# Six groups of seven products in the second layer's FFN, with their weight sums made in HBM by accumulating transfers

## The chip, the core and the metric

The kernel runs on one core of one Trainium2 chip. Its engines are TensorE (PE, and PEld for its weight loads), VectorE (DVE), ScalarE (ACT), GpSimd (POOL) and SyncE (SP), which here only issues transfers; 16 DMA engines carry the transfers of all queues. The metric is the time of one execution on the device in microseconds (us).

## The reference

A decoder of two layers on 256 tokens of width 2048, all in float32. Layer 0 mixes tokens by latent attention of 16 heads, layer 1 by dilated window attention in three groups. Each mixer is followed by an FFN with a convolution over three tokens; the hidden width is 5632, so its first matrix has 2 x 5632 columns, gate and value.

```python
def conv_ffn(h, w_up, conv_w, conv_b, w_down):
    u = h @ w_up
    up = jnp.pad(u, ((0, 0), (CONV_WIDTH - 1, 0), (0, 0)))
    c = conv_b + up[:, 0:S] * conv_w[0]
    for j in range(1, CONV_WIDTH):
        c = c + up[:, j:j + S] * conv_w[j]
    gate, val = c[..., :FFN_HIDDEN], c[..., FFN_HIDDEN:]
    return (jax.nn.silu(gate) * val) @ w_down

for i in range(2):
    x = x + mixer_i(rms_norm(x, attn_norm[i]), ...)
    x = x + conv_ffn(rms_norm(x, ffn_norm[i]), ffn_w_up[i], ffn_conv_w[i], ffn_conv_b[i], ffn_w_down[i])
return rms_norm(x, final_norm)
```

## The kernel before

**Layout.** Features lie on the 128 partitions, tokens along the free axis. The input of a projection is 16 chunks `xs` of 128 features, each a tile of 512 columns: the 256 tokens rounded to the type fp32r (the high part) and beside them what the rounding left (the low part). Weights come from HBM in blocks of 128 output columns: `load` takes a buffer `w` of the pool `wst` (three buffers), issues its transfer on SP's queue, and splits each half of it into `wh` (ScalarE, a copy that rounds) and `wl` (VectorE, the difference), tiles of 128 x 1024 in the pool `wsp` (five buffers). `proj` multiplies a block with 16 chunks: 16 matmuls of 128 x 512 with `wh` and 16 of 128 x 256 with `wl`. That is a *unit*. The helper `unit` issues a projection, then one entry of the list `steps` (small work that is to run in between), then the evacuation of the unit before.

**Norms.** The gain is folded in when `xs` is made; 1/rms is worked out while the first products run. `rstd_x` sums the squares over partitions (TensorE), makes the mean square `ms` (VectorE), and takes its power -0.5 on GpSimd, into `rcol` (L309; `rstd_rank` does so for the ranks of the attention, into `s`, L321). `spread` lays `rcol` out over the partitions by two matmuls into `po` (L296). In the FFN these are the first two entries of `steps`, `col` and `wide`. Apart from the norms GpSimd has a few `memset`s, those of the paddings `upad` of the FFN among them (L802), and at the start some additions.

**The FFN** (`ffn`, run for both layers). The hidden width is 44 blocks `fb`. A plain block takes two units, `up`: gate and value, each a load of 1 MB; the evacuation multiplies with the norm and convolves (`keep`, `conv`). The second matrix is applied in four segments of 10 to 12 blocks (`SEGS`), `down`: 16 units of 640 to 768 KB, each added to the residual. Before each of the last three segments stands a *four* (`SEVEN`, blocks 12, 23 and 34 and the three after each): gate and value of four blocks by seven products instead of eight, in the manner of Strassen and Winograd, over two halves of the tokens, two halves of the input features (each pair of chunks, one even and one odd) and gate against value. Here the tokens are the stationary operand (`xs`, or sums of token and feature halves, `forms`), the weights the moving one, and the results have tokens on the partitions. In each of the 16 steps beside a `down` (`first` and `second`, eight of each), VectorE makes the sums of the weights from one load (`t13`, `t24`; L883 among them) and TensorE runs four or two of the products (L853 to L855, three matmuls for each: high, low, high parts). The product left over (`third`, `s4`) runs in two halves later, and then `turn` transposes the results (16 transposes, L947) and convolves.

**Order.** The program is written in the order above, and Tile's scheduler sets each engine's queue from it by the time at which it takes an instruction to be ready, and by its place in the text. Each queue is run in order.

Of the kernel before, what the change touches and what calls it, by code (L numbers as in the profile page):

```python
# [18 lines left out]
F32 = mybir.dt.float32  # L19
F32R = mybir.dt.float32r  # L20
BF16 = mybir.dt.bfloat16
I32 = mybir.dt.int32
AF = mybir.ActivationFunctionType
# [3 lines left out]
P = 128  # L27
T = 256
# [12 lines left out]
SEGS = ((0, 10), (10, 21), (21, 32), (32, 44))  # L41
HALF = 4 * P
SEVEN = (12, 23, 34)
NEG = -1.0e30


# [6 lines left out]
def trunk_kernel(tc, x_d, pos_d, gain_d, conv_d, const_d, mask_d, wqa_d, wkva_d, wqb_d, wkvb_d, wo_d,  # L53
                 win_d, dwo_d, wup_d, wdn_d, out_d):
    nc = tc.nc
    with ExitStack() as ctx:
# [5 lines left out]
        tab = ctx.enter_context(tc.tile_pool(name="tab", bufs=1))  # L62
        work = ctx.enter_context(tc.tile_pool(name="work", bufs=4))
        small = ctx.enter_context(tc.tile_pool(name="small", bufs=4))
        pp = ctx.enter_context(tc.tile_pool(name="pp", bufs=4, space=PSUM))
        pss = ctx.enter_context(tc.tile_pool(name="pss", bufs=2, space=PSUM))
        pst = ctx.enter_context(tc.tile_pool(name="pst", bufs=1, space=PSUM))
# [3 lines left out]
        def load(src, n, tok=0, cuts=None, after=()):  # L71

            w = wst.tile([P, D], F32, name="w", tag="w")
            cuts = cuts or (0, n)
            for a, b in zip(cuts, cuts[1:]):
                nc.sync.dma_start(w[:, a:b], src[:, a:b])
                if after:
                    after[0]()  # L80
                    after = after[1:]
            parts = []
            for a in range(0, n, WS):
                b = min(n, a + WS)
                wh = wsp.tile([P, WS], F32R, name="wh", tag="wh")
                wl = wsp.tile([P, WS], F32R, name="wl", tag="wl")
                if a < tok:
                    steps = [a] + [c for c in cuts if a < c < b] + [b]
                    for c, e in zip(steps, steps[1:]):
                        h, l = wh[:, c - a:e - a], wl[:, c - a:e - a]  # L90
                        nc.scalar.activation(h, w[:, c:e], AF.Copy)  # L91
                        nc.vector.tensor_sub(l, w[:, c:e], h.bitcast(F32))  # L92
                else:
                    for h, t in enumerate((wh, wl)):
                        src2 = w[:, a + h * WS // 2:a + (h + 1) * WS // 2].rearrange("p (k c) -> p k c", c=T)
                        t4 = t.rearrange("p (k s c) -> p k s c", s=2, c=T)
                        nc.scalar.activation(t4[:, :, 0, :], src2, AF.Copy)
                        nc.vector.tensor_sub(t4[:, :, 1, :], src2, t4[:, :, 0, :].bitcast(F32))
                parts.append((wh, wl))
            return parts  # L100
# [87 lines left out]

        pending = []
        steps = []  # L190

        def nothing():
            pass
# [9 lines left out]
        def unit(project, evacuate):  # L203
            ps = project()
            if steps:
                steps.pop(0)()
            flush()
            pending.append((evacuate, ps))

        def joined(ps):  # L210

            t = work.tile([P, T], F32, name="lo", tag="lo", bufs=2)
            nc.scalar.activation(t, ps[:, T:], AF.Copy)  # L213
            u = work.tile([P, T], F32, name="sum", tag="tmp")
            nc.vector.tensor_add(u, ps[:, :T], t)  # L215
            return u
# [75 lines left out]
        def spread(col, name, pool):  # L292

            ps = pso.tile([P, 512], F32, name="po", tag="po")
            for tt in range(2):
                nc.tensor.matmul(ps[:, ts(tt, P)], col[:, tt:tt + 1].to_broadcast([P, P]), ident,  # L296
                                 start=True, stop=True)
            if pool is None:
                return ps[:, :T]
            t = pool.tile([P, T], F32, name=name, tag=name)  # L300
            nc.vector.tensor_copy(t, ps[:, :T])
            return t

        def rstd_x(paired=False, last=None):
            ps = sumsq("x", paired, last)
            ms = small.tile([P, 2], F32, name="ms", tag="ms")
            nc.vector.tensor_scalar(ms, ps, 1.0 / D, EPS, op0=ALU.mult, op1=ALU.add)
            r = small.tile([P, 2], F32, name="rcol", tag="rcol")
            nc.gpsimd.tensor_tensor(r, ms, negh, op=ALU.pow)  # L309
            return r  # L310
# [38 lines left out]
        def split_to(dst, src):  # L349

            n = src.shape[-1]
            nc.scalar.activation(dst[:, :n], src, AF.Copy)
            nc.vector.tensor_sub(dst[:, n:], src, dst[:, :n].bitcast(F32))

        def split_act(ps):
            o = act.tile([P, 2 * T], F32R, name="a", tag="a")
            split_to(o, ps)
            return o

        def tokens(k, paired=False):  # L360

            return xt[k].rearrange("p (a e) -> p e a" if paired else "p (e a) -> p e a", e=2)
# [428 lines left out]
            out_proj(dwo_d, os, G_FFN + KC, onto=True)  # L791


        def ffn(layer, goff, ready):
            gl = {}
            rb = {}
# [227 lines left out]
            flush()  # L1024


        with tc.tile_pool(name="lat0", bufs=1) as lat, tc.tile_pool(name="att0", bufs=2) as att:
            mla()
        with tc.tile_pool(name="ffn0", bufs=1) as fpool:
# [11 lines left out]
            nc.scalar.activation(xt[c], xt[c], AF.Copy, scale=gains[:, G_FIN + c:G_FIN + c + 1])  # L1041

        with tc.tile_pool(name="ffn1", bufs=1) as fpool:
            ffn(1, G_FFN + KC, final)

        zero = work.tile([P, T], F32, name="zero", tag="lo", bufs=2)
        nc.vector.memset(zero, 0.0)
# [93 lines left out]
```

## Time and profile before

| | |
|---|---|
| device time, median of 3 runs | 2675.28 us (2674.98 to 2675.42) |
| span of the profiled execution | 2673.9 us |
| its own time outside that span | about 1.4 us by the median |
| TensorE busy | 2657.8 us (99%) |
| VectorE busy | 2105.5 us (79%) |
| ScalarE busy | 1639.7 us (61%) |
| GpSimd busy | 24.7 us (1%) |
| transfers of SP's queue | 503.46 MB, 54.9% of the 16 DMA engines' span |

The busy time of an engine is a share of the whole span. The granted clock of TensorE is full in all of the 40 slices. A row of the timeline gives start, duration, engine, line, operation, its output and inputs with shapes and count, and in brackets the engine's idle time before it and what released it. For a stretch of time the busy time of PE, PEld, DVE, ACT and POOL is given in this order, and then the granted clock, the busy share of the DMA engines and the GB/s that they moved.

### The profile page before, as it was taken

Reading aid. Unit: us, or ns where it says so; the run is one execution under the profiler, and the core shown is the slowest. Engines: PE = TensorE matmul, PEld = TensorE weight load, DVE = VectorE, ACT = ScalarE, POOL = GpSimd, SP = SyncE. Lnnn points to the kernel's source line nnn. Section 1 sums busy time; section 2 is a strip of 40 time slices with the busy share of each in tenths; the row PEclk is TensorE's granted clock in tenths of the full one; section 3 lists DMA queues with packets and bytes.
Section 4 is the critical chain, followed back from the end, with each engine's and each line's share of the span. In section 5 each row is a group of like instructions: output and inputs, shape, how many; then the busy total and the mean of one; then the engine's idle time right before and its main releaser. Section 6 shows DMA issues by size and latency. Waiting matters only on the chain.

```text
span 2673.9 us, 40017 instructions
## 1 busy us (share of the span) xinstructions
PE 2657.8 (99%) x15167; PEld 2338.4 (87%) x15167; DVE 2105.5 (79%) x3630; ACT 1639.7 (61%) x2624; POOL 24.7 (1%) x39
## 2 busy tenths in 40 slices
PE   9999999999999999999999999999999999999998
PEld 7998888888888888898888888888888888888887
DVE  7987888898898876676577667667688889889885
ACT  6775666676666764444454444445666667666665
POOL 2000000000000000000000000000000000000000
PEclk9999999999999999999999999999999999999999
DMA  6335555656566565544544544544555575755744
GB/s 246 138 133 203 189 182 193 239 179 224 197 202 227 182 206 198 179 171 170 191 170 164 197 161 174 188 174 160 189 189 175 191 249 171 223 205 189 237 169 147
DMA packets 153553, 506.19 MB, mean 189 GB/s; under 512 B 11024, under 2 KB 86160, under 8 KB 118928
## 3 DMA queue, kind: packets, MB, share of 16 engines
q1 hardware_dynamic: 153072, 503.46, 54.9%
q8 instruction: 119, 1.95, 0.3%
q14 instruction: 74, 0.61, 0.1%
q10 hardware_dynamic: 288, 0.18, 0.0%
HBM read 501.50 MB, written 2.10 MB: 188 GB/s over the span
## 4 chain that ended last, share of the span: by engine, by line
PE 95%; DMA 1%; DVE 1%; issue 0%; ACT 0%; SPq 0%; DVEq 0%; ACTq 0%
PE pp L137 70%; PE pp L165 3%; PE pp L167 3%; PE pp L166 3%; PE ps L855 1%; PE ps L853 1%; PE ps L854 1%; DMA w<-in_wup 1%; PE pp L104 1%; PE pp L106 1%; PE pp L105 1%; PE pp L853 1%; PE pp L854 1%; PE pp L855 1%; PE po L781 1%; PE ps L744 1%
## 5 line engine op out<-in xcount | busy, mean ns | idle before, releaser
L92 DVE TENSOR_TENSOR wl<-w,wh 128x1024 fp32r<-128x1024 f32 (+3 forms) x802 | 881.9, 1110 | 371.0 <-ACT wh L91 228.1
L91 ACT ACTIVATE wh<-w 128x1024 fp32r<-128x1024 f32 (+3 forms) x802 | 770.9, 966 | 370.8 <-PE pp L137 220.7
L137 PE MATMUL pp<-xs,wh 128*128 128x512 f32 x3648 | 855.5, 390 | 0.0
L137 PEld LDWEIGHTS pp<-xs,wh 128*128 128x128 f32 x3648 | 677.1, 188 | 135.8 <-DVE xs L266 0.2
L137 PE MATMUL pp<-xs,wl 128*128 128x256 f32 x3648 | 465.3, 284 | 0.0
L137 PEld LDWEIGHTS pp<-xs,wl 128*128 128x128 f32 x3648 | 455.7, 191 | 9.3
L137 PE MATMUL pp<-a,wh 128*128 128x512 f32 x1920 | 459.7, 390 | 0.0
L137 PEld LDWEIGHTS pp<-a,wh 128*128 128x128 f32 x1920 | 357.7, 188 | 72.6
L137 PEld LDWEIGHTS pp<-a,wl 128*128 128x128 f32 x1920 | 248.1, 191 | 10.2
L137 PE MATMUL pp<-a,wl 128*128 128x256 f32 x1920 | 252.8, 283 | 0.0
L155 DVE TENSOR_TENSOR wl<-w,wh 128x1024 fp32r<-128x1024 f32 x96 | 116.2, 1218 | 62.3 <-ACT wh L154 50.3
L154 ACT ACTIVATE wh<-w 128x1024 fp32r<-128x1024 f32 x96 | 101.6, 1059 | 96.5 <-PE pp L166 50.0
L213 ACT ACTIVATE lo<-pp 128x256 f32<-128x256 f32 x225 | 85.7, 381 | 119.5 <-PE pp L137 119.4
L165 PE MATMUL pp<-wh,xs 128*128 128x512 f32 x384 | 150.0, 391 | 0.0
L167 PE MATMUL pp<-wl,xs 128*128 128x512 f32 x384 | 149.5, 389 | 0.0
L166 PE MATMUL pp<-wh,xs 128*128 128x512 f32 x384 | 149.4, 389 | 0.0
L962 DVE SCALAR_TENSOR_TENSOR cv<-upad,convs,cv 128x256 f32<-128x256 f32 x256 | 121.1, 481 | 18.3 <-ACT cv L958 15.9
L958 ACT ACTIVATE cv<-upad,convs 128x256 f32<-128x256 f32 x128 | 76.4, 598 | 72.7 <-DVE upad L972 71.0
L215 DVE TENSOR_TENSOR sum<-pp,lo 128x256 f32<-128x256 f32 x225 | 94.1, 418 | 0.2
L120 ACT ACTIVATE pp<-x 128x512 f32<-128x512 f32 x144 | 85.1, 591 | 13.6 <-DVE sum L215 6.8
L880 ACT ACTIVATE wh<-w 128x1024 fp32r<-128x1024 f32 x48 | 51.0, 1062 | 60.0 <-PE pp L137 43.0
L167 PEld LDWEIGHTS pp<-wl,xs 128*128 128x128 f32 x384 | 72.1, 188 | 15.0
(299 smaller groups left out, 3154.7 us busy)
## 6 DMA issues: line engine op xcount, KB each, us to landing
w<-in_wup SPq DMA_DIRECT2D x128, 1024.0 KB, 4.8
w<-in_win SPq DMA_DIRECT2D x96, 1024.0 KB, 4.8
w<-in_wup SPq DMA_DIRECT2D x96, 512.0 KB, 5.1
w<-in_win SPq DMA_DIRECT2D x96, 512.0 KB, 4.1
w<-in_wdn SPq DMA_DIRECT2D x64, 704.0 KB, 4.1
w<-in_wdn SPq DMA_DIRECT2D x32, 768.0 KB, 4.2
w<-in_wdn SPq DMA_DIRECT2D x32, 640.0 KB, 5.3
w<-in_wo SPq DMA_DIRECT2D x16, 1024.0 KB, 4.7
```

The costliest lines, as they stand in the source:

```text
L91: nc.scalar.activation(h, w[:, c:e], AF.Copy)
L92: nc.vector.tensor_sub(l, w[:, c:e], h.bitcast(F32))
L120: nc.scalar.activation(dst, chunk.unsqueeze(1).to_broadcast([P, 2, 2, P]), AF.Copy, scale=0.5)
L137: nc.tensor.matmul(ps[:, i * T:], w_k, xs[k][:, :(2 - i) * T], start=(k == 0 and i == own), stop=(k == n - 1), skip_group_check=(i != own))
L154: nc.scalar.activation(wh4, src, AF.Copy)
L155: nc.vector.tensor_sub(wl4, src, wh4.bitcast(F32))
L165: nc.tensor.matmul(ps, xh, wh, start=k == 0, stop=False)
L166: nc.tensor.matmul(ps, xl, wh, start=False, stop=False)
L167: nc.tensor.matmul(ps, xh, wl, start=False, stop=k == KC - 1)
L213: nc.scalar.activation(t, ps[:, T:], AF.Copy)
L215: nc.vector.tensor_add(u, ps[:, :T], t)
L962: nc.vector.scalar_tensor_tensor(o, v, convs[:, cw + j:cw + j + 1], o, op0=ALU.mult, op1=ALU.add)
```

## The change

Layer 0 keeps `ffn`. Layer 1 gets a function of its own, `ffn_ahead`, with twice as many fours.

- **Fours and units.** Six fours, at blocks 12 and 16, 23 and 27, 34 and 38 (`PERIODS`); 12 blocks by units at the start (`FIRST`), and 20 to 22, 31 to 33, 42 and 43 by units between. So 24 units of `up` become three more fours.
- **Halves of a product.** The feature halves are now the lower and the upper eight chunks. Each of the seven products is made on its own, in two halves: `product(i, q)` issues one load of 1 MB (four blocks, 512 columns each, so pieces of 2 KB), four splits, and 12 matmuls of 128 x 512. Its accumulator is one of the two of `ps`. The order is 1, 2, 6, 7, 4, 5, 3, and the results are added into `u` as they come (`use`). `slot` runs what the tables `first`, `downs` and `ups` have for the place after a unit: one half each in the last 12 units of the start, then beside the units of `down`, in the second and third periods 2, 3, 2, 2 halves after the first four.
- **The sums of weights** are read from HBM. For each four, `plan_sums` takes four HBM tiles `t1` to `t4` of 2.1 MB and lists 16 copies of 0.524 MB from `wup` into them and 16 transfers of the same size that add to what is there (`accum_op`): 96 of each in all. `some_ahead`, called at the start of each `load`, hands out one entry at two of five calls after the eighth: a copy on SP's queue, an accumulating transfer, six entries behind its copy, on GpSimd's, in pieces of at most 256 elements.

The diff, cut to what the parts below speak of:

```diff
+FIRST = 12
+PERIODS = ((0, 11, 12, 16, (20, 21, 22)), (11, 22, 23, 27, (31, 32, 33)), (22, 33, 34, 38, (42, 43)))
...
+        hbm = ctx.enter_context(tc.tile_pool(name="hbm", bufs=1, space=bass.MemoryType.DRAM))
...
 def load(src, n, tok=0, cuts=None, after=()):
+            some_ahead()
             w = wst.tile([P, D], F32, name="w", tag="w")
...
+        def plan_sums(layer, fours):
+            copies, adds = [], []
+            for fb0 in fours:
+                t = {i: hbm.tile([4, P, WS], F32, name=f"t{i}_{layer}_{fb0}") for i in (1, 2, 3, 4)}
+                made[layer, fb0] = t
+                last = None
+                for f in range(4):
+                    blk = lambda h, j: wup_d[layer, 2 * (fb0 + f) + h, :, j * WS:(j + 1) * WS]
+                    copies += [(t[i][f], blk(*hj)) for i, hj in ((1, (0, 0)), (3, (1, 1)), (2, (1, 1)), (4, (0, 1)))]
+                    adds += [(t[1][f], blk(1, 0)), (t[3][f], blk(1, 0)), (t[2][f], t[1][f])]
+                    if last:
+                        adds.append(last)
+                    last = (t[4][f], t[2][f])
+                adds.append(last)
+            late = 6
+            for n in range(len(copies) + late):
+                ahead.append((copies[n] if n < len(copies) else None, adds[n - late] if n >= late else None))
+
+        def some_ahead():
+            state["loads"] = state.get("loads", 0) + 1
+            if state["loads"] > 8 and state["loads"] % 5 in (0, 3) and ahead:
+                c, a = ahead.pop(0)
+                if c:
+                    nc.sync.dma_start(*c)
+                if a:
+                    nc.gpsimd.dma_start(*a, accum_op=ALU.add, max_dma_last_dim=WS)
...
+            products = {1: ("a11", (0, 0)), 2: ("a12", (0, 1)), 3: ("s4", (1, 1)), 4: ("a22", 4), 5: ("s1", 1),
+                        6: ("s2", 2), 7: ("s3", 3)}
...
+                def product(i, q):
...
+                    w = wst.tile([P, D], F32, name="w", tag="w")
+                    if isinstance(what, int):
+                        src = t[what][:, :, q * HALF:(q + 1) * HALF]
+                    else:
+                        h, j = what
+                        src = wup_d[layer, 2 * fb0:2 * fb0 + 8].rearrange("(f i) p c -> i f p c", i=2)[h]
+                        src = src[:, :, j * WS + q * HALF:j * WS + (q + 1) * HALF]
+                    nc.sync.dma_start(w.rearrange("p (f c) -> p f c", f=4), src.rearrange("f p c -> p f c"))
...
+                if s == 0:
+                    deal(m, first[12:], [1] * 12)
+                    deal(m, downs[0], (1, 1))
+                else:
+                    put(ups[s - 1], 0, m.pop(0))
+                    put(ups[s - 1], 2, m.pop(0))
+                    deal(m, ups[s - 1][3:], (1, 1, 1))
+                    deal(m, downs[s], (2, 3, 2, 2))
...
+        plan_sums(1, [fb for _, _, one, two, _ in PERIODS for fb in (one, two)])
...
-            ffn(1, G_FFN + KC, final)
+            ffn_ahead(1, G_FFN + KC, final)
```

The queues as they are built. GpSimd's queue before, from the norm of layer 0's input (`rcol_536`) over the two norms of the ranks to that of layer 0's FFN (`rcol_3656`); a name ends in the number of its tile:

```order
L309 TENSOR_TENSOR rcol_536<-ms_534,negh_115 128x2 [waits DVE_49]
L321 TENSOR_TENSOR s2_546<-ms_543,negh_115 128x2 [waits DVE_49]
L321 TENSOR_TENSOR s2_759<-ms_756,negh_115 128x2 [waits DVE_49]
L802 MEMSET upad0_3600 128x2 [waits DMAHW6_49,PE_49,Activation_49]
L802 MEMSET upad1_3602 128x2
L802 MEMSET upad2_3604 128x2
L802 MEMSET upad3_3606 128x2
L309 TENSOR_TENSOR rcol_3656<-ms_3654,negh_115 128x2 [waits DVE_49]
```

The same place in the changed kernel begins so. DMAHW are counters of SP's transfers, DMASW of GpSimd's own:

```order
L344 TENSOR_TENSOR rcol_562<-ms_560,negh_117 128x2 [waits DVE_49]
L225 DMA t1_1_12_119<-in_wup 128x4x256 [waits DMAHW6_49]
L356 TENSOR_TENSOR s2_572<-ms_569,negh_117 128x2 [waits DVE_49]
L225 DMA t3_1_12_121<-in_wup 128x4x256 [waits DMAHW0_49]
L225 DMA t2_1_12_120<-t1_1_12_119 512x256 [waits DMAHW2_49,DMASW0_49]
L225 DMA t1_1_12_119<-in_wup 128x4x256 [waits DMAHW4_49]
L225 DMA t4_1_12_122<-t2_1_12_120 512x256 [waits DMAHW3_49,DMASW2_49]
L356 TENSOR_TENSOR s2_785<-ms_782,negh_117 128x2 [waits DVE_49]
```

and ends so, at the norm of layer 0's FFN, which is now `rcol_3700`:

```order
L225 DMA t2_1_34_136<-t1_1_34_135 512x256 [waits DMAHW0_49,DMASW0_49]
L225 DMA t4_1_34_138<-t2_1_34_136 512x256 [waits DMAHW2_49,DMASW3_49,DMASW2_49]
L225 DMA t1_1_34_135<-in_wup 128x4x256 [waits DMAHW4_49]
L225 DMA t3_1_34_137<-in_wup 128x4x256 [waits DMAHW5_49,DMASW5_49]
L225 DMA t2_1_34_136<-t1_1_34_135 512x256 [waits DMAHW7_49,DMASW4_49]
L225 DMA t4_1_34_138<-t2_1_34_136 512x256 [waits DMAHW1_49,DMASW7_49,DMASW6_49]
L225 DMA t1_1_34_135<-in_wup 128x4x256 [waits DMAHW2_49]
L344 TENSOR_TENSOR rcol_3700<-ms_3698,negh_117 128x2 [waits DVE_49]
```

Between the two pieces stand further transfers of this kind, 73 in all ahead of `rcol_3700` (the memsets of `upad` among them, behind 50); the other 23 follow it.

SP's queue before, from the last heads' weights over the out projection to the first `down` of layer 0; xN stands for N alike in a row:

```order
L78 DMA w<-in_wqb 128x1536
L78 DMA w<-in_wkvb 128x2048
L78 DMA w<-in_wo 128x2048 x6
L798 DMA convs<-in_conv 128x352
L78 DMA w<-in_wo 128x2048 x10
L78 DMA w<-in_wup 128x2048 x24
L78 DMA w<-in_wdn 128x1280
```

A part of the same out projection in the changed kernel:

```order
L82 DMA w_2758<-in_wo 128x2048
L223 DMA t1_1_23_127<-in_wup 128x1024
L223 DMA t3_1_23_129<-in_wup 128x1024
L82 DMA w_2816<-in_wo 128x2048
L223 DMA t2_1_23_128<-in_wup 128x1024
L223 DMA t4_1_23_130<-in_wup 128x1024
L223 DMA t1_1_23_127<-in_wup 128x1024
L82 DMA w_2871<-in_wo 128x2048
```

Two or three copies stand between each weight load and the next; all 96 stand between the first head and the units of layer 0's FFN: 36 beside the heads, 31 beside the out projection, 29 beside the FFN's first units.

SP's queue in layer 1's FFN before, beside the second segment of `down`:

```order
L78 DMA w<-in_wdn 128x1408
L873 DMA w<-in_wup 128x4x256 x2
L78 DMA w<-in_wdn 128x1408 x2
L873 DMA w<-in_wup 128x4x256 x2
L78 DMA w<-in_wdn 128x1408 x2
```

and in the changed kernel:

```order
L899 DMA w_23255<-t2_1_23_128 128x4x512
L82 DMA w_23281<-in_wdn 128x1408
L899 DMA w_23328<-t2_1_23_128 128x4x512
L899 DMA w_23351<-t3_1_23_129 128x4x512
L82 DMA w_23374<-in_wdn 128x1408
L899 DMA w_23411<-t3_1_23_129 128x4x512
L899 DMA w_23434<-t4_1_23_130 128x4x512
L899 DMA w_23457<-t4_1_23_130 128x4x512
L82 DMA w_23479<-in_wdn 128x1408
```

One load (two transfers) for two units of `down` became two or three loads for each; four of the seven products read their weights from the tiles `t`, three from `wup`.

193 lines of the change are left out of this document (added).

## The prediction

> **What bounds the kernel now.** I read the page's sums and its chain first, to see which engine's work sets the end, and then the busy time by stretches, for what the transfers have left over.
>
> ```profile
> span 2673.9 us, 40017 instructions
> PE 2657.8 (99%) x15167; PEld 2338.4 (87%) x15167; DVE 2105.5 (79%) x3630; ACT 1639.7 (61%) x2624; POOL 24.7 (1%) x39
> q1 hardware_dynamic: 153072, 503.46, 54.9%
> PE 95%; DMA 1%; DVE 1%; issue 0%; ACT 0%; SPq 0%; DVEq 0%; ACTq 0%
> ```
>
> PE is busy for 99% of the span and carries 95% of the chain: a column of products less is time less, as long as nothing else comes to be late. GpSimd does nothing (24.7 us). All transfers of weight are on one queue, SP's.
>
> ```profile
> 20.00:25.00 5.00, 5.00 (x31) 4.41 (x31) 5.00 (x6) 3.74 (x8) 2.96 (x4) 1.00 1.03 414
> 41.00:272.00 231.00, 229.36 (x1640) 215.27 (x1639) 190.60 (x502) 154.22 (x367) 3.31 (x7) 1.00 0.46 164
> 2100.00:2106.00 6.00, 6.00 (x33) 5.16 (x32) 5.05 (x9) 4.17 (x7) 0.00 (x0) 1.00 0.95 305
> 2426.00:2520.00 94.00, 94.00 (x498) 81.17 (x497) 80.72 (x103) 64.62 (x92) 0.00 (x0) 1.00 0.66 215
> ```
>
> The last two columns are the busy share of the 16 DMA engines and the GB/s. The most that they move when full is 414 GB/s (whole 8 KB rows); in pieces of 1 KB it is 305 at a share of 0.95, so 321. From the first head's weights (41 us) to the start of layer 0's FFN (272 us) they move 164 GB/s. This stretch is where the change puts most of its new transfers.
>
> What waits there on GpSimd's queue:
>
> ```profile
> 44.91 0.82 POOL L309 TENSOR_TENSOR rcol<-ms,negh 128x2 f32<-128x2 f32 x1 [11.63 <-DVE ms L307]
> 64.19 1.59 POOL L321 TENSOR_TENSOR s<-ms,negh 128x2 f32<-128x2 f32 x1 [13.49 <-DVE ms L319]
> 186.78 0.20 POOL L802 MEMSET upad<- 128x2 f32 x4 [120.99 <-ACT a L352]
> 272.03 1.61 POOL L309 TENSOR_TENSOR rcol<-ms,negh 128x2 f32<-128x2 f32 x1 [85.06 <-DVE ms L307]
> ```
> ```profile
> 273.61 3.82 PE L137 MATMUL pp<-xs,wh 128*128 128x512 f32 x16
> 277.26 0.61 PE L296 MATMUL po<-cst,rcol 128*128 128x128 f32 x4
> ```
> ```profile
> 40.26 0.33 SPq L78 DMA_DIRECT2D w<-in_wqb  x1
> 44.79 0.33 SPq L78 DMA_DIRECT2D w<-in_wkvb  x1
> ```
>
> GpSimd computes 1/rms of layer 0's FFN input (rcol) from 272.03 to 273.64; TensorE, in order, spreads it at 277.26, after the second unit. So rcol may be 3.6 us late and no more; then PE stands.
>
> **The change, part by part.** First what it takes from PE, by rows of layer 1's FFN: two units, a first and a second step of a four, a quarter of its seventh product, eight of the 16 transposes of its turns, the one gap, and a unit of down.
>
> ```profile
> 2002.32 7.44 PE L137 MATMUL pp<-xs,wh 128*128 128x512 f32 x32
> ...
> 2013.44 7.44 PE L137 MATMUL pp<-xs,wh 128*128 128x512 f32 x32
> ...
> 2076.12 0.40 PE L853 MATMUL ps<-wh,xs 128*128 128x512 f32 x1
> ...
> 2078.86 2.43 PE L137 MATMUL pp<-a,wh 128*128 128x512 f32 x10
> ...
> 2082.32 0.40 PE L853 MATMUL pp<-wh,forms 128*128 128x512 f32 x1
> ...
> 2083.71 2.43 PE L137 MATMUL pp<-a,wh 128*128 128x512 f32 x10
> ```
> ```profile
> 2154.84 0.50 PE L855 MATMUL ps<-wl,xs 128*128 128x512 f32 x1 [0.72 <-DVE wl L883]
> ...
> 2173.53 0.39 PE L853 MATMUL ps<-wh,forms 128*128 128x512 f32 x1
> ...
> 2176.25 3.79 PE L137 MATMUL pp<-xs,wh 128*128 128x512 f32 x16
> ...
> 2206.76 0.60 PE L947 MATMUL pt<-cst,t 128*128 128x128 f32 x4
> ...
> 2207.55 2.15 PE L137 MATMUL pp<-xs,wl 128*128 128x256 f32 x16
> ...
> 2247.40 2.66 PE L137 MATMUL pp<-a,wh 128*128 128x512 f32 x11
> ...
> 2251.20 0.40 PE L853 MATMUL ps<-wh,xs 128*128 128x512 f32 x1
> ```
>
> A unit takes (2013.44 - 2002.32) / 2 = 5.56 us. By the starts of the rows a first step takes 2078.86 - 2076.12 = 2.74, a second 2083.71 - 2082.32 = 1.39, the quarter 2176.25 - 2173.53 = 2.72, the eight transposes 2207.55 - 2206.76 = 0.79, and a unit of down 2251.20 - 2247.40 = 3.80. An old four takes 8 x (2.74 + 1.39) + 2 x 2.72 + 2 x 0.79 = 40.1. A new four is 14 half products of 12 matmuls, each like the quarter above: 14 x 2.72 + 1.6 = 39.7. Before, the layer has 3 fours and 24 units where after it has 6 fours: 3 x 40.1 + 24 x 5.56 = 253.7 against 238.2, so **15.5 us less**, all on PE's path. VectorE no longer makes the sums of weights in this layer, and with that goes the one gap of 0.7 us: 16.2 in all. Taking other tiles for u, the order of the seven and the forms made closer together moves work on VectorE and ScalarE, which have 21% and 39% free: nothing.
>
> Second, the loads of layer 1's FFN. A half product needs 1.05 MB in 2.72 us of PE. Where the plan sets nine of them beside four units of down (3.80 us and 0.72 MB each), that is 12.3 MB in 39.7 us, 310 GB/s, against 215 in the old stretch; pieces are now 2 KB. By the 414 of whole rows there is room, by the 305 of 1 KB pieces it is 0.7 us short in each of the three stretches. If each stretch also loses one landing (4.8 us below), it is 14. I take 4, between nothing and 14, and nearer the first, since the ring of three buffers is full when a stretch starts.
>
> ```profile
> w<-in_wup SPq DMA_DIRECT2D x128, 1024.0 KB, 4.8
> w<-in_win SPq DMA_DIRECT2D x96, 512.0 KB, 4.1
> ```
>
> Third, the sums in HBM: 96 copies of 0.524 MB on SP's queue and 96 accumulating transfers of the same size on GpSimd's. The text asks for two per five loads; the queues as built have them elsewhere. On SP two or three copies stand behind each weight load from the first head on; on GpSimd 73 accumulating transfers stand ahead of layer 0's rcol, which only DVE's mean square released before. Each waits for the copy, or the sum, that it reads, and 73 copies stand on SP up to the one that the last of them reads. So rcol cannot run before these have gone through the 16 engines: 35.0 MB of weights, 73 copies (38.3 MB), and the 72 accumulating transfers ahead of the last (37.7 MB).
>
> Costs. Weights: 35.0 MB at 414 GB/s, 85 us. A copy: 1.27 us at 414; the trace has none from HBM to HBM, so its ends are this one pass and two, 2.53; I take one, since a load too is read and written once. An accumulating transfer: the trace has none; it reads source and destination, so between one pass at 414 (1.27) and two at the 321 of its 1 KB pieces (3.27); I take two at 414, 2.53, which lies nearest the middle of both rows. Together 85 + 92 + 182 = 359 us, from 41 us on: the last stands issued at 400, rcol ends at 401.6, and PE, which spread it at 277.3, waits **124 us**. With one pass for everything: 85 + 92 + 91, at 309, 33 us. With two passes for copies, two at 321 for the others and the weights at 355 (164 / 0.46): 99 + 185 + 235, at 560, 284 us. The stretch was full of PE's work before, so nothing hides this; and whether PE loses it earlier, to weight loads that stand behind copies in one queue, or at the spread, changes the place and not the sum, since the engines have the same bytes to move. The second norm on that queue, at 64.19, now has five accumulating transfers ahead of it; what it loses is inside the 124. The memsets of upad, too, stand behind 50 of them and are inside.
>
> By the fit that the Trainium skill's page "DMA: Bandwidth & Descriptors", section "Anatomy of one DMA — SWDGE (gpsimd) path", gives for GpSimd's queue (2.0 us and the bytes at 436 GB/s), one such transfer is an estimate of 3.2 us, 72 one after another 231, the last is issued at 272, nothing waits, and the sum would be 2663. The trace's 512 KB loads land after 4.1 us, 0.9 more, and no row shows an accumulating one.
>
> Behind rcol remain 23 copies and 23 accumulating transfers beside 20 units: 29 + 58 us and 20 x 2.53 of loads, 138 us, in 20 x 5.56 = 111. On SP's queue alone it is 80, which fits, and the rest may be late without harm, its first reader being 1.5 ms away; ends 0 and 27, I take 5. In the rest of the program nothing is moved.
>
> The sum against the profiled execution: 2673.9 - 16.2 + 4 + 124 + 5 = 2790.7 of span, and 1.4 as the median of the runs (2675.3) stands above that span: **2792 us**.
>
> **Rivals.** The first ends faster: *the new transfers are hidden*. It needs the engines to move from HBM to HBM beside the loads more than they ever move here. The deciding point is the rate: 35.0 + 38.3 + 37.7 = 111 MB by 275.7 us, in 235 us, 473 GB/s, with each accumulating transfer counted once. For it speaks that the engines stood free for 54% of that stretch; against it the row of 414 at a share of 1.03. Then 2673.9 - 16.2 + 4 + 1.4 = 2663. The rule of the page named above would have it so. The same page, section "Issuing engines are not separate DMA queues", lets all queues share the 16 engines; no run here shows two at once.
>
> The second: *an accumulating transfer costs no more than a copy*. PE then waits 33 us, and the time is 2673.9 - 16.2 + 33 + 1.4 = 2692.
>
> The third: *both cost more*, two passes for the copy and the slow pieces for the rest: 2673.9 - 16.2 + 284 + 27 + 14 + 1.4 = 2984.
>
> **How the numbers follow.** My forecast, two passes for the accumulating transfers, gets 0.60; one pass 0.15; both dear 0.11; hidden 0.14. Predicted is the likeliest, 2792. The range runs from 2680 to 2965: below it lies hidden (0.14), above it half of the dear case. About 0.2% (5 us) is what a measurement can tell. Slower by that: forecast, dear, and nearly all of one pass, 0.85; within it: the shallow end of hidden, 0.02; faster: the rest of hidden, 0.13.
>
> **What would show it.** In the profile of the changed kernel: GpSimd's rcol of layer 0 starts near 400 us instead of 272, with PE idle at the spread or, before it, for weights in attention and out-projection; DMA shares near 1 from 45 us to there, in place of 0.46; after about 500 us each stage as long as before; layer 1's FFN some 12 us shorter, halves of 2.72 us each. The forecast is wrong if the DMA share stays well under 1 while accumulating transfers are in flight (then GpSimd's own issue, or the landing of each one, sets the pace), if rcol starts at 272 (hidden), or if layer 1's FFN is no shorter because its product loads are late.

## The result, and the profile after

The changed kernel takes 2921.2 us (median of 4 runs, 2915.2 to 2925.5) against 2675.35: a ratio of 1.092, 95% interval 1.090 to 1.093. It is 246 us slower, where 117 were forecast. The profiled execution has a span of 2913.5, 239.6 longer than before.

The page's sums, the two queues and the chain (a queue's columns: packets, MB, share of the 16 engines over the span):

```profile
span 2913.5 us, 39943 instructions
PE 2669.2 (92%) x14950; PEld 2331.8 (80%) x14951; DVE 2084.6 (72%) x3568; ACT 1663.6 (57%) x2651; POOL 136.2 (5%) x135
q1 hardware_dynamic: 169776, 585.25, 57.4%
q0 software_dynamic: 50688, 50.34, 11.6%
PE 76%; DMA 14%; DVE 4%; issue 3%; ACT 2%; POOL 1%; SPq 0%; DVEq 0%; ACTq 0%; POOLq 0%
```

TensorE is busy for about as long as before (2669 us for 2658) but idle for 8% of the span, and transfers carry 14% of the chain. GpSimd's timeline shows where, by the norms, which cut the program into its stages:

```profile
497.43 1.01 POOL L225 DMA_DIRECT2D t<-t  x1 [5.07 <-DMA t<-t]
498.07 1.68 POOL L225 DMA_DIRECT2D t<-in_wup  x1
498.87 1.63 POOL L344 TENSOR_TENSOR rcol<-ms,negh 128x2 f32<-128x2 f32 x1
...
1236.78 1.64 POOL L344 TENSOR_TENSOR rcol<-ms,negh 128x2 f32<-128x2 f32 x1 [556.07 <-DVE ms L342]
...
2187.52 1.61 POOL L344 TENSOR_TENSOR rcol<-ms,negh 128x2 f32<-128x2 f32 x1 [88.77 <-DVE ms L342]
2903.28 0.69 POOL L344 TENSOR_TENSOR rcol<-ms,negh 128x2 f32<-128x2 f32 x1 [714.15 <-DVE ms L342]
```

and the same norms before, behind the one of layer 0's FFN at 272.03:

```profile
993.99 1.61 POOL L309 TENSOR_TENSOR rcol<-ms,negh 128x2 f32<-128x2 f32 x1 [720.35 <-DVE ms L307]
...
1944.72 1.61 POOL L309 TENSOR_TENSOR rcol<-ms,negh 128x2 f32<-128x2 f32 x1 [88.75 <-DVE ms L307]
2663.57 0.69 POOL L309 TENSOR_TENSOR rcol<-ms,negh 128x2 f32<-128x2 f32 x1 [717.23 <-DVE ms L307]
```

Layer 0's rcol starts 226.8 us later, straight behind a transfer and with no idle time of its own. From it to the next norm it takes 737.9 us for 722.0, then 950.7 for 950.7, and layer 1's FFN 715.8 for 718.9: 226.8 + 16.0 + 0 - 3.1 = 239.7, the whole difference. TensorE's timeline at the spread:

```profile
325.86 3.81 PE L141 MATMUL pp<-xs,wh 128*128 128x512 f32 x16
500.56 1.22 PE L331 MATMUL po<-cst,rcol 128*128 128x128 f32 x4 [170.88 <-POOL rcol L344]
```

It comes 223.3 us later than before (277.26): TensorE stood for 170.9 us at this place, and lost the rest in the attention and the out projection. The engines' share in that stretch, in the columns of the prediction's table, with the part in which nothing but accumulating transfers ran:

```profile
41.00:499.00 458.00, 248.65 (x1671) 229.46 (x1669) 196.37 (x510) 155.38 (x372) 88.32 (x81) 0.78 1.02 257
```
```profile
350.00:498.00 148.00, 0.00 (x0) 0.00 (x0) 0.00 (x0) 0.00 (x0) 42.86 (x41) 0.50 0.94 135
```

A share of 1.02 for 458 us leaves next to nothing free, at only 257 GB/s. In the second stretch GpSimd issues 37 transfers, and the bytes moved are those of 38: 3.9 us each, 135 GB/s at a share of 0.94.

### The profile page after: what moved, and what is told of

Same layout as the page of the kernel before. It is cut to its first block, busy times and chain, and to the rows that moved or that the text cites. A ratio compares the mean times of both kernels' runs of the same rounds, so it can differ in the third digit from the quotient of the medians.

```text
span 2913.5 us, 39943 instructions
## 1 busy us (share of the span) xinstructions
PE 2669.2 (92%) x14950; PEld 2331.8 (80%) x14951; DVE 2084.6 (72%) x3568; ACT 1663.6 (57%) x2651; POOL 136.2 (5%) x135
## 4 chain that ended last, share of the span: by engine, by line
PE 76%; DMA 14%; DVE 4%; issue 3%; ACT 2%; POOL 1%; SPq 0%; DVEq 0%; ACTq 0%; POOLq 0%
PE pp L141 53%; DMA t<-t 3%; DMA t<-in_wup 3%; PE pp L169 3%; PE pp L171 3%; PE pp L170 3%; PE ps L911 3%; PE ps L912 3%; PE ps L913 3%; DMA w<-in_wup 2%; DMA w<-in_wo 2%; DVE wl L96 1%; DMA w<-in_wkvb 1%; POOL t L225 1%; DMA w<-in_wqb 1%
## 5 line engine op out<-in xcount | busy, mean ns | idle before, releaser
L96 DVE TENSOR_TENSOR wl<-w,wh 128x1024 fp32r<-128x1024 f32 x754 | 823.2, 1103 | 380.2 <-ACT wh L95 254.8
L95 ACT ACTIVATE wh<-w 128x1024 fp32r<-128x1024 f32 x754 | 718.6, 959 | 417.2 <-PE pp L141 207.5
L141 PE MATMUL pp<-xs,wh 128*128 128x512 f32 x3264 | 769.5, 391 | 7.0 <-DVE xs L301 7.0
L141 PEld LDWEIGHTS pp<-xs,wh 128*128 128x128 f32 x3264 | 607.2, 188 | 130.0 <-DVE xs L301 7.9
L141 PE MATMUL pp<-a,wh 128*128 128x512 f32 x1920 | 465.7, 393 | 4.3 <-ACT wh L95 4.1
L141 PE MATMUL pp<-xs,wl 128*128 128x256 f32 x3264 | 419.3, 284 | 2.9 <-DVE wl L96 2.9
L141 PEld LDWEIGHTS pp<-xs,wl 128*128 128x128 f32 x3264 | 410.8, 192 | 12.4 <-DVE wl L96 3.1
L906 DVE TENSOR_TENSOR wl<-w,wh 128x1024 fp32r<-128x1024 f32 x168 | 202.7, 1222 | 57.1 <-ACT wh L905 48.7
L905 ACT ACTIVATE wh<-w 128x1024 fp32r<-128x1024 f32 x168 | 173.6, 1055 | 85.1 <-DMA w<-t 41.8
L159 DVE TENSOR_TENSOR wl<-w,wh 128x1024 fp32r<-128x1024 f32 x96 | 116.2, 1218 | 62.3 <-ACT wh L158 51.4
L1237 ACT ACTIVATE cv<-upad,convs 128x256 f32<-128x256 f32 x64 | 38.1, 597 | 214.5 <-DVE upad L1251 214.2
L331 PE MATMUL po<-cst,rcol 128*128 128x128 f32 x20 | 3.8, 317 | 170.9 <-POOL rcol L344 170.9
L158 ACT ACTIVATE wh<-w 128x1024 fp32r<-128x1024 f32 x96 | 101.6, 1059 | 96.5 <-PE pp L170 49.9
L248 ACT ACTIVATE lo<-pp 128x256 f32<-128x256 f32 x201 | 76.3, 380 | 106.5 <-PE pp L141 106.3
```

The lines of the kernel that those rows point to most:

```text
L141: nc.tensor.matmul(ps[:, i * T:], w_k, xs[k][:, :(2 - i) * T], start=(k == 0 and i == own), stop=(k == n - 1), skip_group_check=(i != own))
L158: nc.scalar.activation(wh4, src, AF.Copy)
L159: nc.vector.tensor_sub(wl4, src, wh4.bitcast(F32))
L905: nc.scalar.activation(as4(wh), w5[:, 2 * h:2 * h + 2], AF.Copy)
L906: nc.vector.tensor_sub(as4(wl), w5[:, 2 * h:2 * h + 2], as4(wh).bitcast(F32))
```

## The experiments

Times are medians; "before" is the same kernel on the same chip, 2675.0 to 2675.4. L344 is the power of the norm and takes L309's part (L340 in the kernel with no sums, which is four lines shorter there). The edits are to the changed kernel unless another is named.

**Layer 1's FFN alone** (no_sums).

```diff
-                c, a = ahead.pop(0)
-                if c:
-                    nc.sync.dma_start(*c)
-                if a:
-                    nc.gpsimd.dma_start(*a, accum_op=ALU.add, max_dma_last_dim=WS)
+                ahead.pop(0)
...
-                    if isinstance(what, int):
-                        src = t[what][:, :, q * HALF:(q + 1) * HALF]
...
+                    h, j = (0, 0) if isinstance(what, int) else what
...
```

> Left out: all copies and all accumulating transfers; the products 4 to 7 read plain blocks of the up weights where they would read sums. What is left of the change is layer 1's FFN. My account so far (all of the loss up to layer 1's FFN comes from the transfers of the sums, and that FFN gains 3.1 us by the distance between the norms before and behind it, not the 12 I forecast, since PE stands 7.6 us at two transposes and at the last segment): rcol of layer 0's FFN starts at 272 us as before, the same three gaps stay, and the time is 2675.4 - 3.1, about 2672. Rival (the three gaps are an after-effect of the sums, for instance of where the scheduler put things): no gaps, 2663.

2675.6 us (2671.8 to 2680.7, 10 runs), ratio 1.000 (0.999 to 1.001). GpSimd's norms in its profile:

```profile
271.62 1.62 POOL L340 TENSOR_TENSOR rcol<-ms,negh 128x2 f32<-128x2 f32 x1 [85.05 <-DVE ms L338]
993.97 1.61 POOL L340 TENSOR_TENSOR rcol<-ms,negh 128x2 f32<-128x2 f32 x1 [720.73 <-DVE ms L338]
1944.70 1.61 POOL L340 TENSOR_TENSOR rcol<-ms,negh 128x2 f32<-128x2 f32 x1 [88.77 <-DVE ms L338]
2659.36 0.69 POOL L340 TENSOR_TENSOR rcol<-ms,negh 128x2 f32<-128x2 f32 x1 [713.05 <-DVE ms L338]
```

All of the loss ahead of layer 1's FFN is that of the sums. The FFN itself gains 4.2 us in this profile and nothing in the median, which was not expected: its runs scatter by 9 us where those of before scatter by 3. Gaps of TensorE remain (3.7 us at the last segment, 1.4 and 0.3 at transposes).

**Copies without the adding** (no_adds).

```diff
-                if a:
-                    nc.gpsimd.dma_start(*a, accum_op=ALU.add, max_dma_last_dim=WS)
```

> Left out: the 96 accumulating transfers; the 96 copies stay where the scheduler put them, ahead of the first units of layer 0's FFN, and the products 4 to 7 read the unsummed copies. By the price of copies as in the prediction (1.27 us of the engines each): 35.0 MB of weights and 73 copies need 85 + 92 = 177 us in the 231 us up to rcol, so rcol is at most some us late and the whole loses only what single weight loads lose behind two or three copies in one queue; 2672 + 0 to 15 us. Rival (the copies are as dear as two passes, 2.53 us): 85 + 185 = 270 us, rcol 40 us late, 2710. Second rival (the loss of before the rcol, some 45 us of PE gaps up to 329 us, is all from loads behind copies): 2715.

2672.8 us, ratio 0.999 (0.998 to 1.000). The stretch up to rcol, and SP's queue, of this kernel and of the one with no sums:

```profile
41.00:272.00 231.00, 229.98 (x1646) 215.86 (x1645) 190.72 (x500) 154.73 (x368) 3.92 (x8) 1.00 0.94 330
```
```profile
q1 hardware_dynamic: 169776, 585.25, 63.6%
```
```profile
q1 hardware_dynamic: 155952, 534.92, 58.5%
```

The copies cost nothing: TensorE is as busy as before (229.98 and 229.36 of 231), with the engines' share doubled to 0.94. Their price is (0.636 x 2669.0 - 0.585 x 2670.0) / 96 = 1.41 us.

**The adding in the text's order** (adds_paced). `keep_in_program_order` pins an instruction behind what the text has before it on its queue.

```diff
-                    nc.gpsimd.dma_start(*a, accum_op=ALU.add, max_dma_last_dim=WS)
+                    tc.keep_in_program_order(nc.gpsimd.dma_start(*a, accum_op=ALU.add, max_dma_last_dim=WS))
```

> Nothing left out. Each accumulating transfer is pinned on GpSimd's queue behind what the program's text has there before it: 6 instead of 73 stand ahead of layer 0's rcol, 51 fall into layer 0's FFN and 39 into the dilated attention's projection. The copies stay hoisted. Theory Q (the loss is the order of GpSimd's queue: rcol waits for 73 accumulating transfers, each 3.5 us of all 16 engines): rcol starts within 20 us of 272, PE's wait of 171 us is gone, and the time is that of the kernel without these transfers plus at most 10 us, 2672 to 2700. Theory C (the loss is contention: wherever the 96 transfers run, 338 us of engine time, loads come late): at least a third of it stays, above 2780.

2733.8 us, ratio 1.021 (1.020 to 1.023): between the two theories, so neither holds alone. The norms of layer 0's FFN and of the layer behind it:

```profile
274.38 1.63 POOL L344 TENSOR_TENSOR rcol<-ms,negh 128x2 f32<-128x2 f32 x1 [83.62 <-DMA w<-in_wup]
1058.68 1.64 POOL L344 TENSOR_TENSOR rcol<-ms,negh 128x2 f32<-128x2 f32 x1 [489.92 <-DVE ms L342]
```

The wait at the spread is gone (rcol at 274 for 499), so it came from rcol's place in GpSimd's queue. But layer 0's FFN now takes 784.3 us, 62 more than before: what runs beside it is not hidden.

**Both in the text's order** (paced): the copies are pinned in the same way.

> Nothing left out. Copies and accumulating transfers are both pinned behind what the text has before them on their queues: two of each per five weight loads, 12 copies ahead of the first load of layer 0's FFN instead of 67, 63 ahead of the dilated projection, 33 in it. Theory Q: five loads take 27.8 us of PE and 12.7 us of the engines, two copies 2.5 and two accumulating transfers 7.0 us, a share of 0.80: everything is hidden, and the time is that of layer 1's FFN alone, 2672, or 2675 with a few late loads. Theory C: loads come late in each stage from 60 to 1300 us, above 2700.

2703.6 us, ratio 1.011 (1.009 to 1.012), 28 us above before: loads come late, as theory C has it, but not in each stage. By the norms all of it lies in layer 0's FFN:

```profile
271.79 1.63 POOL L344 TENSOR_TENSOR rcol<-ms,negh 128x2 f32<-128x2 f32 x1 [83.63 <-DVE ms L342]
1029.29 1.64 POOL L344 TENSOR_TENSOR rcol<-ms,negh 128x2 f32<-128x2 f32 x1 [70.63 <-DVE ms L342]
...
1980.03 1.64 POOL L344 TENSOR_TENSOR rcol<-ms,negh 128x2 f32<-128x2 f32 x1 [88.75 <-DVE ms L342]
```
```profile
PE pp L141 <- DVE wl L96: 12.2, 7, 3.0
PE ps L1134 <- DVE wl L1162: 12.1, 9, 3.2
```

757.5 us there instead of 722.0, and 950.7 in the dilated attention, with 39 accumulating transfers in it, as before. TensorE's waits (total, times, longest) are for splits: of whole loads (L96) and of the loads of the fours in 1 KB pieces (L1162). VectorE in turn waits 65.3 us for loads of the fours to land in this FFN (line L1160), 9.9 before. The mean share of the engines (last but one), which I had set at 0.80, was 0.88 in the 722 us from 272 on, for 0.60 before the change:

```profile
272.00:994.00 722.00, 696.91 (x3814) 602.15 (x3814) 593.59 (x922) 464.88 (x735) 60.64 (x52) 0.99 0.88 263
```

There was room in the mean, and the loads still came late.

**Plain transfers in place of the adding** (plain_adds), and **pieces of 4 KB** (big_pieces).

```diff
-                    nc.gpsimd.dma_start(*a, accum_op=ALU.add, max_dma_last_dim=WS)
+                    nc.gpsimd.dma_start(*a, max_dma_last_dim=WS)               # plain_adds
+                    nc.gpsimd.dma_start(*a, accum_op=ALU.add, max_dma_last_dim=4 * WS)   # big_pieces
```

> Left out: the adding. The 96 transfers on GpSimd's queue stay with their sources, destinations, pieces of 1 KB, places and waits, but overwrite instead of adding. In the changed kernel one accumulating transfer holds the 16 engines for 3.5 us (its queue's 11.6% of 2913.5 us, by 96). Theory A (the add itself is the price): as plain transfers they cost 1.3 us at 414 GB/s to 1.6 at the 321 of 1 KB pieces, so 85 + 92 + 72 x 1.3 to 1.6 = 270 to 292 us after 41: rcol at 310 to 335 us instead of 499, and 2710 to 2750 in all. Rival (the chain on GpSimd's queue, where each waits for the landing of the one that it reads, whatever the engines do): rcol stays beyond 450, and the time above 2850.

> Nothing left out. The accumulating transfers go in pieces of 4 KB instead of 1 KB; their bytes, order and waits stay. Theory P (the small pieces are a good part of the 3.5 us): the price falls to two passes at 414, 2.5 us, rcol comes 72 x 1.0 us earlier, at about 430, and the time is 2850. Rival (the price goes by bytes that are added, not by pieces): rcol stays at 499 within 15 us, 2900 to 2930.

plain_adds 2817.2 us (ratio 1.053, 1.051 to 1.055), big_pieces 2891.8 (1.081, 1.079 to 1.083): each lies between its theory and the rival. GpSimd's queue and rcol, first of plain_adds, then of big_pieces:

```profile
q0 software_dynamic: 13824, 50.34, 5.7%
```
```profile
397.28 0.64 POOL L225 DMA_DIRECT2D t<-t  x1 [3.26 <-DMA t<-t]
...
398.70 0.73 POOL L344 TENSOR_TENSOR rcol<-ms,negh 128x2 f32<-128x2 f32 x1
```
```profile
q0 software_dynamic: 13824, 50.34, 9.5%
```
```profile
455.16 1.33 POOL L344 TENSOR_TENSOR rcol<-ms,negh 128x2 f32<-128x2 f32 x1
```

The packets show that the plain transfers went in pieces as long as the big ones (3.6 KB on average, for 1.0 in the changed kernel), against what I had written; so the three make a ladder. By share, span and count a transfer holds the engines for 1.67 us plain (0.057 x 2816.9 / 96), 2.86 adding in 4 KB pieces, 3.52 adding in 1 KB pieces. Of the 1.85 us by which an accumulating transfer is dearer than a plain one, 1.19 is the add and 0.66 the small pieces. The price hardly depends on the place: by the same working it is 3.39 in adds_paced and 3.55 in paced.

The rival of the chain on GpSimd's queue has a part too: with plain transfers rcol came at 399, well behind the 335 expected. From 363 to 398 us SP's queue issued one load and one copy at its very start and nothing more, TensorE stood at the spread, and the engines' share was only 0.64, while a transfer of one sum into another waited on GpSimd for the sum that it reads to land (the row at 397.28). There the landings, not the engines, set the pace.

**Nothing that TensorE needs on GpSimd's queue** (norms_off_queue).

```diff
-            nc.gpsimd.tensor_tensor(r, ms, negh, op=ALU.pow)
+            nc.vector.tensor_scalar(r, ms, 0.05, None, op0=ALU.min)
...
-                nc.gpsimd.memset(u[:, 0:2], 0.0)
+                nc.vector.memset(u[:, 0:2], 0.0)
```

The norms of the ranks (`s`) and the memsets of both FFNs are changed in the same way.

> Left out: the power of the norms (VectorE takes a minimum of the mean square and a constant in its place); the paddings' memsets are on VectorE too. So GpSimd's queue holds nothing that TensorE needs, while copies and accumulating transfers stand where the changed kernel has them. Theory Q (171 us of the loss is the place of one small instruction in a queue): no wait at the spread; the transfers go on beside layer 0's FFN, and the time is that of the kernel with only the transfers of GpSimd pinned, 2734, plus what the attention lost to them (about 45 us): 2740 to 2790. Rival (the engines are the bound whatever waits for them, weights 106 us + 73 copies of 1.41 + 72 adds of 3.52 = 462 us of engine time from 41 us on): TensorE loses the same time to late weights instead, 2880 or more.

2801.9 us (ratio 1.047, 1.045 to 1.049), a little above the range of theory Q. What takes the norm's place, on VectorE:

```profile
322.48 0.16 DVE L344 TENSOR_SCALAR rcol<-ms 128x2 f32<-128x2 f32 x1
```
```profile
1123.31 0.16 DVE L344 TENSOR_SCALAR rcol<-ms 128x2 f32<-128x2 f32 x1
```

So of the 246 us, 119 go with the place of a few small instructions in a queue. The other 127 remain: 50 up to rcol (322 for 272) and 79 in layer 0's FFN (800.8 us), where TensorE's largest waits are again for splits of loads (22.8 us at the fours, 16.1 at whole loads). Full engines alone are thus not what set the time: with the same transfers in the same order, and nothing that TensorE needs behind them on GpSimd's queue, the loss is half as large.

**Paced, in pieces of 4 KB** (paced_big): the edit of big_pieces on the paced kernel.

> Nothing left out. The paced kernel (2703.6 us, all of its loss of 35 us beside layer 0's FFN) with pieces of 4 KB instead of 1 KB in the accumulating transfers, which in the hoisted order lowered their price from 3.52 to 2.86 us of the engines. If the price decides what the loads of layer 0's FFN lose: 35 x 2.86 / 3.52 = 28 or less, 2690 to 2697. Rival (it is the number of transfers in the way of a load, not their length): 2703 as before. Second rival (longer pieces hold each engine longer, and a load's pieces wait behind them): above 2710, as layer 0's FFN from its norm to the next took 755 us with the big pieces and 738 with the small ones in the hoisted order.

2704.0 us (ratio 1.011, 1.009 to 1.012): as with the small pieces, so the first rival fits. What a load loses beside these transfers did not follow their price; whether it follows their number was not tried.

**No sums beside layer 0's FFN** (not_in_ffn0), on the paced kernel:

```diff
-            if state["loads"] > 8 and state["loads"] % 5 in (0, 3) and ahead:
+            if state["loads"] > 8 and state["loads"] % 5 in state.get("when", (0, 3)) and ahead:
...
+            state["when"] = ()
             ffn(0, ...)
+            state["when"] = (0, 1, 2, 3)
```

> Nothing left out. Copies and accumulating transfers pinned in the text's order as in the paced kernel, and none is handed out beside layer 0's FFN: 11 or 12 of each beside the attention and its out projection, 77 beside the dilated attention's projection (four per five of its whole-block loads), the rest after it. The paced kernel lost 35 us, all between rcol of layer 0's FFN and the next norm, with 25 us of PE gaps beside the segments of down, and nothing in the dilated projection with 39 accumulating transfers in it. Theory: only where a stretch has little room for its own loads (the downs with fours of layer 0) do the transfers cost anything; with none there the time is that of the kernels without sums, 2671 to 2677. Rival (twice as many in the dilated projection is too much: 77 x 4.8 = 370 us of engine time beside a share of 0.46 in 860 us, 0.89 in all): loads come late there, 2690 or more.

2675.5 us (2671.3 to 2678.2, 10 runs), ratio 1.000 (0.999 to 1.001). The dilated attention's projection in this kernel, and the same stretch before:

```profile
994.00:1856.00 862.00, 861.92 (x4811) 754.98 (x4811) 592.32 (x1101) 411.37 (x555) 101.72 (x87) 1.00 0.94 277
```
```profile
994.00:1856.00 862.00, 861.93 (x4812) 755.11 (x4811) 591.77 (x1099) 411.63 (x555) 1.81 (x5) 1.00 0.51 177
```

With 80 of the 96 copies and 86 of the 96 accumulating transfers issued in this one stretch, TensorE is busy for 861.92 us, as before. The loss was one of place.

**Turns moved** (better), on the kernel with no sums beside layer 0's FFN: in each period the transposes of the first four come in slots 6 and 7 instead of 5 and 6; only in the last period those of the second four come in slots 1 and 2, where they were in 1 to 3. The half products are dealt out to fit.

> Nothing left out. As the kernel with no sums beside layer 0's FFN, and in layer 1's FFN the transposes of the first four of a period one place later (slots 6 and 7 instead of 5 and 6), those of the last four one place earlier (slots 1 and 2). If the three PE gaps there (2 + 2 + 3.7 us, and about 1.7 us of half clock behind each of 2 us or more) come from transposes and gated blocks that ScalarE has ready too late, they go, and the time is 5 to 10 us under that of the kernel beside it: 2663 to 2669. Rival (the loads of the half products are late, and move the gaps only): the same time as the kernel beside it.

2673.4 us, ratio 0.999 (0.998 to 1.000): not told apart from the kernel beside it, whose runs scatter by 7 us. TensorE's waits now name another releaser:

```profile
PE pt L957 <- DVE cv L975: 4.1, 2, 2.9
...
PE pp L141 <- ACT a L387: 2.1, 2, 1.1
```

The third turn writes the accumulator `pt`, from which VectorE is still convolving the first.

**One turn to a slot** (spread_turns), on the kernel with no sums beside layer 0's FFN:

```diff
-                put(downs[s], 5, *turns[:2])
-                put(downs[s], 6, *turns[2:], m.pop(0))
-                deal(m, downs[s][7:], (1, 1, 1, 2, 1, 1, 2, 1, 2))
+                for f in range(4):
+                    put(downs[s], 5 + f, turns[f])
+                put(downs[s], 8, m.pop(0))
+                deal(m, downs[s][9:], (2, 2, 2, 2, 1, 2, 1) if s < 2 else (2, 2, 2, 2, 2, 2))
...
+                # turns2 in slots 1 to 4; in the last period settled in slot 15 of down, in slots 0, 0, 1, 2
```

> Nothing left out. As the kernel with no sums beside layer 0's FFN; in layer 1's FFN each turn has a slot of its own (5 to 8; 1 to 4 behind the second four), and the second four of the last period is done a slot earlier, so that its turns stand in the first three of the last four slots. If the gaps there come from two turns in one slot or in neighbouring ones (the third turn writes the accumulator that VectorE still reads for the first: the waits of the last try named cv, not a load), they go, with the slow clock behind them: 6 to 9 us under the kernel beside it, 2666 to 2669. Rival (two halves for each unit from slot 9 on need more than the engines give beside a down, as 2, 3, 2, 2 did): new gaps at the half products, 2675 or more.

2665.4 us (2662.9 to 2667.1, 5 runs), ratio 0.996 (0.995 to 0.998): 9.5 us faster than before, with every sum made, and a little below the range expected. Its norms around layer 1's FFN, and the longest of TensorE's waits in it:

```profile
1945.26 1.64 POOL L344 TENSOR_TENSOR rcol<-ms,negh 128x2 f32<-128x2 f32 x1 [56.06 <-DVE ms L342]
2651.21 0.68 POOL L344 TENSOR_TENSOR rcol<-ms,negh 128x2 f32<-128x2 f32 x1 [704.31 <-DVE ms L342]
```
```profile
PE pp L141 <- ACT a L387: 1.1, 1, 1.1
```

That FFN takes 706.0 us, 12.9 less than before. The rival's late loads, with two halves to a unit, did not appear.

## Why the prediction was wrong

**The sign and the place held, and the mechanism in part.** rcol of layer 0's FFN stood behind 73 accumulating transfers on GpSimd's queue, TensorE lost its time there and before it, the engines were nearly full from the first head on, and the dilated attention was untouched.

**The term that failed is the 124 us,** which measured 223. Each of its three prices was low. Weights: I took 35.0 MB at the 414 GB/s of whole rows, 85 us, though the row beside it had the price of that stretch's own loads: a share of 0.46 over 231 us, 106, for 37.9 MB. A copy: 1.27, measured 1.41. An accumulating transfer: 2.53, measured 3.52, above even the 3.27 that I had as its upper end. That end came from a row (2100 to 2106) in which SP's queue moved two loads of the fours and two of the downs, so it was not the rate of 1 KB pieces alone.

With the measured prices, 106 + 73 x 1.41 + 72 x 3.52 = 462 us from 41 on, 503; rcol started at 498.9. With the 2.86 of the 4 KB pieces the same sum gives 456, and rcol of that kernel started at 455.2. These prices are shares taken from the same runs, so the agreement says that the engines were full (shares of 1.02 and 1.01 up to rcol), and does not test the prices apart. With 1.67 the sum gives 370, and rcol of the plain one came at 399: its share up to there was 0.95 of 358 us, which is 18 of the 29 us, lost in the chain of landings described above; the rest is open. The changed kernel has the same chain ahead of rcol (the row at 497.43), but with the engines at 0.94 over the last 148 us, by which landings can have cost it some 9 us.

The Trainium skill's page "DMA: Bandwidth & Descriptors", section "Anatomy of one DMA — SWDGE (gpsimd) path", gives 2.0 us and the bytes at 436 GB/s for a transfer on GpSimd's path, by my estimate 3.2 us here: nearer than my 2.53 to the 3.9 of the stretch without other work. The rival that I drew from it failed on the other half of the sum: in that stretch these microseconds hold the 16 engines (a share of 0.94), so hardly anything fits beside them.

**That the sum holds does not make the engines the only bound.** I wrote that the order changes the place of the loss and not the size. norms_off_queue contradicts this: with the same transfers in the same places 119 us went. The transfers, with the engines nearly full, set when the queue came to rcol; that rcol stood behind them at all was the order of the queue.

**The transfers behind rcol:** forecast 5 us up to the next norm, measured 19.5 from the spread on (223.3 to 242.8). I had set all of the engines' time against all of TensorE's; the paced kernel shows that layer 0's FFN, with its fours beside the downs, loses although the stretch has room (a share of 0.88).

**Layer 1's FFN:** forecast 16.2 less and 4 more for loads, measured 3.1 less. Halves were 2.75 us and not 2.72, for 84 of them 2.5 us. Nearly all of the rest went to what I had costed at nothing, the order of products and turns. TensorE's timeline:

```profile
2254.31 0.40 PE L911 MATMUL ps<-wh,xs 128*128 128x512 f32 x1
...
2257.06 3.79 PE L141 MATMUL pp<-xs,wh 128*128 128x512 f32 x16
...
2561.89 0.63 PE L957 MATMUL pt<-cst,t 128*128 128x128 f32 x4 [2.07 <-ACT wh L905]
...
2739.95 0.63 PE L957 MATMUL pt<-cst,t 128*128 128x128 f32 x4 [1.80 <-ACT wh L905]
...
2842.48 0.80 PE L141 MATMUL pp<-a,wl 128*128 128x256 f32 x2 [3.72 <-ACT a L387]
```

The gaps are 7.6 us, and a slow clock follows two of them (below), by the granted clock an estimated 3 us more (1.7 behind the first, and about 1.5 at 0.57 from 2842 to 2846). With the 2.5 us of the halves that is about the 13.1 missing from the 16.2, and hardly anything is left over for late loads: my 4 us were set against the wrong cause. spread_turns shows that the gain was there: 12.9 us once the turns stand apart.

## What to carry to other kernels

A transfer that waits on an engine's in-order queue holds up every small instruction behind it: look, in the queue as built, for what a scheduler has set ahead of the few instructions that the busiest engine needs, and pin what is not urgent. Cost a stage by the share of the DMA engines that its row shows and not by the best GB/s seen, and let the upper end for a new kind of transfer lie well above the dearest row. Room in the mean is not room everywhere: a share of 0.94 cost nothing beside loads of whole blocks, while layer 0's FFN, with fours in small pieces beside the downs, lost at 0.88.

## What was new of the hardware

By its queue's share an accumulating transfer from HBM to HBM held the 16 engines for 3.52 us per 0.524 MB in 1 KB pieces and 2.86 in 4 KB pieces; a plain one on the same queue took 1.67, a copy on SP's queue 1.41.

A gap of about 2 us on TensorE can cost nearly as much again. The granted clock (last but two) in the changed kernel behind the gap of 2.07 us and behind that of 1.80, and in the kernel with no sums at the gap of 3.72 (which ends at 2597.7):

```profile
2562.00:2564.00 2.00, 2.00 (x9) 1.61 (x9) 2.00 (x5) 2.00 (x6) 0.00 (x0) 0.61 0.68 161
2564.00:2566.00 2.00, 2.00 (x6) 1.57 (x5) 2.00 (x6) 1.43 (x3) 0.00 (x0) 0.54 0.93 361
...
2740.00:2742.00 2.00, 2.00 (x11) 1.74 (x12) 2.00 (x5) 2.00 (x5) 0.00 (x0) 1.00 0.54 140
```
```profile
2594.00:2598.00 4.00, 0.29 (x1) 0.29 (x2) 3.29 (x8) 3.26 (x7) 0.00 (x0) 0.74 0.45 148
2598.00:2602.00 4.00, 4.00 (x16) 3.71 (x16) 1.32 (x3) 0.00 (x0) 0.00 (x0) 0.50 0.08 32
```

Behind the first, TensorE works at 0.61 and 0.54 for 4 us, 1.7 us lost; behind the shorter one at full clock; behind the long one at half clock for 4 us or more. The length alone does not decide: in the changed kernel a longer gap, in layer 0's FFN, was followed by full clock (1.00 from 601.4 to 606):

```profile
601.36 1.22 PE L141 MATMUL pp<-xs,wl 128*128 128x256 f32 x8 [2.91 <-DVE wl L96]
```

The Trainium skill's page "TensorE: Matmul & The Clock Gate", section "HAM oscillation — how this bites in real kernels", warns of gaps above some 3.4 us; here a slow clock followed one of 2.07. A slow clock that follows such a gap in one run and not in another would fit the scatter between runs of these kernels, which was not tested by itself.
